# HGRN2 pairs in one tile of two PSUM banks, block states for both heads, alternating sums, and the query norm beside epsilon

## The chip, the cores and the metric

The kernel runs on one core of a Trainium2 chip, as one launch. The metric is the device time of an execution in microseconds; where several executions were timed, their median. Engines are named as in the profile: PE is TensorE (matmul), DVE is VectorE, ACT is ScalarE, POOL is GpSimd and SP is SyncE, which issues most transfers.

## What is computed

A trunk of two layers over 512 positions of width 1024, all in float32. Each layer is a half-step feed-forward block (FFN), a mixer, and a second FFN; a final norm follows.

```python
for layer in range(DEPTH):
    x = x + 0.5 * swiglu(rmsnorm(x, norm_ffn1[layer]), ffn1_gate[layer], ffn1_up[layer], ffn1_down[layer])
    x = x + hybrid_mixer(rmsnorm(x, norm_mix[layer]), ...)
    x = x + 0.5 * swiglu(rmsnorm(x, norm_ffn2[layer]), ffn2_gate[layer], ffn2_up[layer], ffn2_down[layer])
```

The mixer projects x once and runs three kinds of heads on the result. HGRN2 has four heads of key width 64 and value width 64, the gated delta net (GDN) four heads of width 128, and RG-LRU a recurrence over 256 channels:

```python
# HGRN2: S_t = diag(f_t) S_{t-1} + k_t v_t^T (k = 1 - f), o_t = S_t^T q_t
scores = jnp.einsum('bhtd,bhsd,bhtsd->bhts', qi, ki, decay)
o = jnp.einsum('bhts,bhsv->bhtv', scores, vi) + jnp.einsum('bhtd,bhdv->bhtv', qi * jnp.exp(cum), state)
# GDN: the query is scaled to unit length, the output to unit mean square
cq = l2norm(cq) * (GD_DK ** -0.5)
o_gd = o_gd * lax.rsqrt(jnp.mean(o_gd * o_gd, axis=-1, keepdims=True) + EPS) * gd_norm_w * silu(gd_z)
# RG-LRU: two gates of a block-diagonal product, then a scan
r = sigmoid(einsum(xb, wr) + br);  ig = sigmoid(einsum(xb, wi) + bi)
```

## The kernel before

Everything lies transposed, channels in the 128 partitions and the 512 positions (S) in the columns, in four blocks of 128 positions (NJ = 4). A wide product takes a 128x128 weight block against 512 columns into one PSUM bank. To keep float32 accuracy at the fast rate each weight is split into a high part (`whi`, a cast on ACT, L176) and a low part (`wlo`, a difference on DVE, L177), and each step is three products (L212 to L214).

PSUM has eight banks, handed out under three tags: "mm" (three), "mx" (three) and "hx" (two). `bank()` takes the next bank of a tag, in the order in which the program asks, so a request waits for an earlier request of its tag. `rstd` (L293) sums squares on PE and `spread` (L304) spreads a row over the partitions with a product; both take "hx", as do the FFN's down products.

An FFN multiplies gate tiles (mm) and up tiles (mx) and then down tiles. In the very first, the first gate and the first up tile are asked for together and multiplied in turn, k by k, as the pieces of x come in. Which instruction stands where is decided by a tile scheduler, from dependencies and estimated costs, except on PE within the mixer: there the order is written out by a slot scheduler of the kernel (`Slots`), which sets the products of small steps (HGRN2, GDN, RG-LRU) between the wide products of the projection. An engine works its instructions off in order, so a PE instruction that waits holds up all behind it.

HGRN2 works on pairs of heads (two pairs, i = 0 and 1), a head's 64 key rows in each half of the partitions. Scores between positions are built by levels (`hgrn_level`, H = 0, 1, 2, 4, ..., 64): at each level q and k are multiplied with decays (L993, L994), the products of all four blocks are formed for both heads (L1009 for the masked levels, else L1022; e is the head, each has a bank of "hx"), and the part of the result that belongs to the level is copied into the head's score matrix `SD`, by a predicated copy per head on DVE (L1013). `hgrn_state` forms the state products (L1046, the heads alternating between column halves of one bank) and the states at the block starts. `hgrn_sum` adds scores times values (L1064) and state times query (L1067), all blocks of one head and then of the other:

```python
for e in range(2):
    for j in range(NJ):
        m = nc.tensor.matmul(po[r, js], lhsT=V[:, j, vs], rhs=d["SD"][e][:, j, :], ...)
        if j:
            m = nc.tensor.matmul(po[r, js], lhsT=st[r, j - 1, :], rhs=d["q"][r, js], ...)
```

`rglru` forms for each i = 0 and 1 two gate products (L1163), each in a bank of its own, with a Sigmoid on ACT behind each (L1164). `gdn_core` forms the decay masks `DT` with four products (L637) and an Exp each (L639).

Of the kernel before, what the change touches and what calls it, by code (L numbers as in the profile page):

```python
# [112 lines left out]
class Trunk:  # L113
# [14 lines left out]
    def bank(self, tag="mm", shape=(P, S)):  # L128
        return self.tile(self.pp, shape, F32, tag, 2 if tag == "hx" else 3)
# [159 lines left out]
    def rstd(self, j0, n, tag="hx"):  # L289
# [9 lines left out]
    def spread(self, rt, n, tag="hx"):  # L299
# [10 lines left out]
    def ffn(self, l, f, nxt):  # L310
# [6 lines left out]
        for h in range(3):  # L317
# [4 lines left out]
            for kind, m in ffn_order(h):  # L322
# [191 lines left out]
    def mixer_in(self, l):  # L514
# [7 lines left out]
        pv = [self.bank("mx" if j < 2 else "hx", (P, NV)) for j in range(NJ)]  # L522
# [178 lines left out]
    def gdn_q(self):  # L701
# [5 lines left out]
        self.rq = self.tile(self.mp, (P, 16), F32, "rq")  # L707
        rq = self.small(16, "rq_hc")
        self.rsqrt(rq, qsq.rearrange("p h c -> p (h c)"), 16, 1.0, EPS)
        nc.vector.tensor_copy(self.rq.rearrange("p (c h) -> p h c", h=4), rq.rearrange("p (h c) -> p h c", h=4))  # L710
# [130 lines left out]
    def gdn_core(self):  # L841
# [103 lines left out]
    def in_hf(self, l, i):  # L945
# [3 lines left out]
        def then(ps):  # L949
            if i == 0:  # L950
                d = {t: self.tile(self.mp, (P, n), F32, "hg_" + t)
                     for t, n in (("f", S), ("k", S), ("q", S), ("s0", S), ("s1", S), ("kk", 384), ("st", 192))}
            else:

                v = self.tile(self.mp, (P, 4, S), F32, "gd_v")
                d = {t: v[:, j, :] for j, t in enumerate(("f", "k", "q", "s0"))}
                d.update({t: self.tile(self.mp, (P, n), F32, "hg1" + t) for t, n in (("s1", S), ("kk", 384), ("st", 192))})
            d["SD"] = [d[t].rearrange("p (j t) -> p j t", t=P) for t in ("s0", "s1")]
            d["tot"] = d["f"]
            self.hg[i] = d  # L960
# [19 lines left out]
    def hgrn_level(self, i, H):  # L980
# [3 lines left out]
        q, k = d["q"], d["k"]  # L984
        if H == 1:
            nc.vector.tensor_tensor(q, q, d["f"], ALU.mult)
        elif H > 1:

            nb, h = S // H, H // 2
            tv = d["tot"].rearrange("p (b two) -> p b two", two=2)  # L990
            q4 = q.rearrange("p (b two h) -> p b two h", two=2, h=h)
            k4 = k.rearrange("p (b two h) -> p b two h", two=2, h=h)
            nc.vector.tensor_tensor(q4[:, :, 1, :], q4[:, :, 1, :], bc(tv[:, :, 0], h), ALU.mult)  # L993
            nc.vector.tensor_tensor(k4[:, :, 0, :], k4[:, :, 0, :], bc(tv[:, :, 1], h), ALU.mult)  # L994
            t2 = self.tile(self.mp, (P, 256), F32, "hg_tot", bufs=4)[:, 0:nb]
            nc.vector.tensor_tensor(t2, tv[:, :, 0], tv[:, :, 1], ALU.mult)
            d["tot"] = t2
        if H == P:
            return
        if H in MASKED:  # L1000

            nb = P // (2 * H)
            half = lambda v: v.rearrange("p (j b two h) -> p j b two h", j=NJ, b=nb, two=2)[:, :, :, 1, :]
# [342 lines left out]
```

## Time and profile before

| what | value |
| --- | --- |
| median of three runs | 2093.62 us (2089.04 to 2094.09) |
| profiled execution | 2088.65 us |
| its span, first to last instruction | 2086.6 us |
| PE busy | 2063.3 us, 99% |
| DVE busy | 1118.8 us, 54% |
| ACT busy | 807.2 us, 39% |
| mean granted PE clock | 0.996 |

Span and profiled execution differ by 2.05 us, which lie outside the first and the last instruction. Busy time of PE counts a product that is still running, so 99% means that PE almost never waits, and not that it works at its peak.

### The profile page before, as it was taken

What the parts mean: (1) busy time and instruction counts of PE and PEld (TensorE: products, weight loads), DVE (VectorE), ACT (ScalarE), POOL (GpSimd) and SP (SyncE); (2) the same over time, 40 slices, a digit from 0 to 9 for tenths busy, and PEclk for the clock granted to TensorE, in tenths of its full rate; (3) what the DMA queues carried; (4) which work ended last, traced back from release to release, by engine and by line L of the source; (5) the groups of instructions that cost most, each with busy time, mean ns of one, the idle gap of its engine ahead of it and who ended that gap; (6) DMA issues with size and microseconds to landing.
All of it is one profiled execution on the core that took longest, in us unless ns stands there. A gap on an engine that the chain in (4) does not pass through costs nothing.

```text
span 2086.6 us, 26732 instructions
## 1 busy us (share of the span) xinstructions
PE 2063.3 (99%) x10292; PEld 1676.2 (80%) x10292; DVE 1118.8 (54%) x2100; ACT 807.2 (39%) x1533; POOL 12.6 (1%) x38
## 2 busy tenths in 40 slices
PE   8999999999999999999999999999999999999997
PEld 6888888878888888888888888888788878888886
DVE  6434445786676443444644344457856754444345
ACT  5323223644564332323433232346346543223233
POOL 0000000000000000000000000000000000000000
PEclk9999999999999999999999999999999999999999
DMA  5232232322122222322223323223211222332222
GB/s 185 91 100 93 92 100 76 97 71 57 52 64 92 97 91 94 99 91 96 96 91 92 100 91 99 91 74 101 70 39 62 76 91 96 91 100 93 92 90 71
DMA packets 67488, 184.99 MB, mean 89 GB/s; under 512 B 18976, under 2 KB 21920, under 8 KB 67360
## 3 DMA queue, kind: packets, MB, share of 16 engines
q1 hardware_dynamic: 66128, 182.12, 27.3%
q8 instruction: 81, 1.33, 0.3%
q10 hardware_dynamic: 1232, 1.16, 0.2%
q14 instruction: 47, 0.39, 0.1%
HBM read 180.36 MB, written 2.88 MB: 88 GB/s over the span
## 4 chain that ended last, share of the span: by engine, by line
PE 98%; DVE 1%; DMA 0%; issue 0%; ACT 0%; DVEq 0%; SPq 0%; ACTq 0%
PE mm L212 14%; PE mm L214 14%; PE mm L213 14%; PE mx L212 8%; PE mx L214 8%; PE mx L213 8%; PE hx L212 8%; PE hx L214 8%; PE hx L213 8%; PE hx L1009 1%; PE mx L648 1%; PE hx L1064 1%; PE hx L1067 0%; PE mx L637 0%; PE mx L894 0%; PE mx L782 0%
## 5 line engine op out<-in xcount | busy, mean ns | idle before, releaser
L176 ACT CAST whi<-wraw 128x512 fp32r<-128x512 f32 (+2 forms) x696 | 420.3, 606 | 1001.9 <-PE mm L213 361.7
L177 DVE TENSOR_TENSOR wlo<-wraw,whi 128x512 fp32r<-128x512 f32 (+2 forms) x696 | 464.8, 669 | 347.3 <-ACT whi L176 344.5
L212 PE MATMUL mm<-xh,whi 128*128 128x512 f32 x1120 | 456.0, 407 | 6.7 <-ACT whi L176 6.7
L214 PE MATMUL mm<-xh,wlo 128*128 128x512 f32 x1120 | 442.3, 395 | 0.0
L213 PE MATMUL mm<-xl,whi 128*128 128x512 f32 x1120 | 442.0, 395 | 0.0
L212 PE MATMUL mx<-xh,whi 128*128 128x512 f32 x704 | 278.7, 396 | 0.0
L214 PE MATMUL mx<-xh,wlo 128*128 128x512 f32 x704 | 278.5, 396 | 0.0
L213 PE MATMUL mx<-xl,whi 128*128 128x512 f32 x704 | 276.8, 393 | 0.0
L212 PE MATMUL hx<-y,whi 128*128 128x512 f32 x692 | 272.5, 395 | 0.0
L214 PE MATMUL hx<-y,wlo 128*128 128x512 f32 x692 | 272.3, 393 | 0.0
L213 PE MATMUL hx<-y,whi 128*128 128x512 f32 x692 | 272.1, 393 | 0.0
L212 PEld LDWEIGHTS mm<-xh,whi 128*128 128x128 f32 x1120 | 211.2, 189 | 55.2 <-ACT whi L176 6.7
L214 PEld LDWEIGHTS mm<-xh,wlo 128*128 128x128 f32 x1120 | 211.3, 189 | 50.1 <-DVE wlo L177 0.2
L213 PEld LDWEIGHTS mm<-xl,whi 128*128 128x128 f32 x1120 | 211.9, 189 | 45.9 <-issue 1.4
L214 PEld LDWEIGHTS mx<-xh,wlo 128*128 128x128 f32 x704 | 132.4, 188 | 32.1 <-issue 0.7
L213 PEld LDWEIGHTS mx<-xl,whi 128*128 128x128 f32 x704 | 132.7, 189 | 30.9 <-issue 0.2
L212 PEld LDWEIGHTS mx<-xh,whi 128*128 128x128 f32 x704 | 132.5, 188 | 31.1 <-issue 1.0
L213 PEld LDWEIGHTS hx<-y,whi 128*128 128x128 f32 x692 | 130.2, 188 | 30.9 <-DVE y L236 1.1
L214 PEld LDWEIGHTS hx<-y,wlo 128*128 128x128 f32 x692 | 130.0, 188 | 30.6
L212 PEld LDWEIGHTS hx<-y,whi 128*128 128x128 f32 x692 | 130.0, 188 | 29.5
L359 DVE SCALAR_TENSOR_TENSOR x<-hx,x 128x512 f32<-128x512 f32 x94 | 65.0, 692 | 133.1 <-PE hx L214 133.1
L342 DVE TENSOR_TENSOR fu<-mx,rb 128x512 f32<-128x512 f32 x88 | 60.9, 692 | 139.7 <-PE mx L214 139.7
(325 smaller groups left out, 1779.9 us busy)
## 6 DMA issues: line engine op xcount, KB each, us to landing
wraw<-in_wgu SPq DMA_DIRECT2D x176, 512.0 KB, 3.7
wraw<-in_wd SPq DMA_DIRECT2D x64, 512.0 KB, 3.5
wraw<-in_win SPq DMA_DIRECT2D x52, 512.0 KB, 3.5
wraw<-in_wd SPq DMA_DIRECT2D x32, 384.0 KB, 3.0
wraw<-in_wout SPq DMA_DIRECT2D x16, 512.0 KB, 3.5
wraw<-in_wv SPq DMA_DIRECT2D x8, 264.0 KB, 2.6
x<-in_x SPq DMA_DIRECT2D x3, 512.0 KB, 7.7
out_dram<-xw SPq DMA_DIRECT2D x4, 256.0 KB, 2.5
```

The lines of the kernel that those rows point to most:

```text
L176: self.nc.scalar.copy(hi, raw)
L177: self.nc.vector.tensor_tensor(lo, raw, hi.bitcast(F32), ALU.subtract)
L212: nc.tensor.matmul(ps, lhsT=a, rhs=xh, start=(n == 0), stop=False)
L213: nc.tensor.matmul(ps, lhsT=a, rhs=xl, start=False, stop=False)
L214: nc.tensor.matmul(ps, lhsT=b, rhs=xh, start=False, stop=(n == size - 1))
L342: nc.vector.tensor_tensor(u, pu, rb, ALU.mult)
L359: nc.vector.scalar_tensor_tensor(xm, pd, 0.5, xm, ALU.mult, ALU.add)
L648: self.nc.tensor.transpose(ps[:, c, :], v[:, c * P:(c + 1) * P], self.ident)
L1009: nc.tensor.matmul(banks[e][:, j], lhsT=k[r, j * P:(j + 1) * P], rhs=half(q)[r, j], start=True, stop=True)
L1064: m = nc.tensor.matmul(po[r, js], lhsT=V[:, j, vs], rhs=d["SD"][e][:, j, :], start=True, stop=(j == 0))
```

## The change

Two of the PSUM banks become one tile of two banks, under the tag "hx", of which there is one (`pair()`). All that was in "hx" moves. `rstd`, `spread` and half of the FFN's down products go to "mx", the other half to "mm". HGRN2's two heads lie in the two halves of the pair tile, so that one predicated copy serves both heads at each level; q and k share one tile and are decayed by one multiplication; both heads' score matrices share one tile. The states become block diagonal, 128x128 for both heads, zeroed by POOL, and the sums go block by block, the heads in turn, with one state product for both. RG-LRU's two gate products of one i go into the two halves of a pair tile. GDN's query norm is not taken as a reciprocal root of its own; its square sum joins the output's as an epsilon under one root (`qe`).

```diff
     def bank(self, tag="mm", shape=(P, S)):
-        return self.tile(self.pp, shape, F32, tag, 2 if tag == "hx" else 3)
+        return self.tile(self.pp, shape, F32, tag, 3)
+
+    def pair(self):
+
+        return self.tile(self.pp, (P, 2, S), F32, "hx", 1)
...
-    def rstd(self, j0, n, tag="hx"):
+    def rstd(self, j0, n, tag="mx"):
...
-    def spread(self, rt, n, tag="hx"):
+    def spread(self, rt, n, tag="mx"):
...
-                    pd = self.bank("hx")
+                    pd = self.bank(("mm", "mx")[mt % 2])
...
-        self.rsqrt(rq, qsq.rearrange("p h c -> p (h c)"), 16, 1.0, EPS)
-        nc.vector.tensor_copy(self.rq.rearrange("p (c h) -> p h c", h=4), rq.rearrange("p (h c) -> p h c", h=4))
+        self.qe = self.tile(self.mp, (P, 16), F32, "qe")
+        nc.vector.tensor_scalar(self.qe.rearrange("p (c h) -> p h c", h=4), qsq, EPS, P * P * EPS, ALU.add, ALU.mult)
...
-        nc.vector.tensor_tensor(osq, osq, self.rq, ALU.mult)
-        nc.vector.tensor_tensor(osq, osq, self.rq, ALU.mult)
+        nc.vector.tensor_tensor(osq, osq, self.qe, ALU.add)
         ro = self.tile(self.mp, (P, 16), F32, "ro")
-        self.rsqrt(ro, osq, 16, 1.0 / P / P, EPS, float(np.float32(P ** -0.5)))
-        nc.vector.tensor_tensor(ro, ro, self.rq, ALU.mult)
+        self.rsqrt(ro, osq, 16, 1.0 / P, 0.0)
...
-            banks = [self.bank("hx", (P, NJ, nb, H)) for _ in range(2)]
+            pt = pt[:, :, 0:P // 2].rearrange("p g (b h) -> p g b h", h=H)
             for j in range(NJ):
                 for e in range(2):
                     r = slice(64 * e, 64 * e + 64)
-                    nc.tensor.matmul(banks[e][:, j], lhsT=k[r, j * P:(j + 1) * P], rhs=half(q)[r, j],
+                    nc.tensor.matmul(pt[:, NJ * e + j], lhsT=k[r, j * P:(j + 1) * P], rhs=half(q)[r, j],
                                      start=True, stop=True)
-            for e in range(2):
-                sd = half(d["SD"][e].rearrange("p j t -> p (j t)"))
-                nc.vector.copy_predicated(sd, lv[:, None].to_broadcast([P, NJ, nb, H]), banks[e])
+            nc.vector.copy_predicated(half(sd), lv[:, None].to_broadcast([P, 2 * NJ, nb, H]), pt)
...
+        po = self.pair()[:, 0, :]
+        for j in range(NJ):
+            js = slice(j * P, (j + 1) * P)
+            for e in range(2):
+                r = slice(64 * e, 64 * e + 64)
+                nc.tensor.matmul(po[r, js], lhsT=V[:, j, (2 * i + e) * 64:(2 * i + e) * 64 + 64], rhs=sd[:, e, j, :],
+                                 start=True, stop=(j == 0))
+            if j:
+                nc.tensor.matmul(po[:, js], lhsT=st[:, j - 1, :], rhs=d["q"][:, js], start=False, stop=True)
...
+            pr = self.pair()
             for n, cb, s in ((0, C_BR, r[:, i, :]), (1, C_BI, ig)):
-                ps = self.bank("hx")
+                ps = pr[:, n, :]
                 nc.tensor.matmul(ps, lhsT=self.rgw[:, l, n, i, :], rhs=xc, start=True, stop=True)
                 nc.scalar.activation(s, ps, AF.Sigmoid, bias=col(cb + i))
```

How the built programs differ is seen in the order of an engine's instructions. A row gives the line, the operation, what is written and read, and the shape of what is written; some rows name in brackets the engines for whose semaphores the instruction waits. Lines are those of each kernel itself: a product of L212 to L214 before is one of L216 to L218 now.

The first piece is PE at the gate products of RG-LRU in the first layer (hx are their banks, tmp is the input, rgw the weights). Before:

```order
L882 MATMUL mx_916_4794<-gt_913_4769,Kn_593_3079 128x128 [waits Activation_49] x4
L894 MATMUL mx_918_4801<-gt_913_4769,DT_610_3162 128x128 x4
L1163 MATMUL hx_921_4813<-tmp_903_4726,rgw_6_89 128x512 [waits DVE_49]
L1163 MATMUL hx_922_4816<-tmp_903_4726,rgw_6_89 128x512
L212 MATMUL mm_923_4821<-xh_7_91,whi_907_4743 128x512
```

and now:

```order
L887 MATMUL mx_888_4726<-gt_885_4701,Kn_592_3078 128x128 [waits Activation_49] x4
L899 MATMUL mx_890_4733<-gt_885_4701,DT_609_3161 128x128 x4
L1171 MATMUL hx_893_4745<-tmp_875_4658,rgw_6_89 128x512 [waits DVE_49]
L1171 MATMUL hx_893_4745<-tmp_875_4658,rgw_6_89 128x512 [waits Activation_49]
L216 MATMUL mm_894_4752<-xh_7_91,whi_879_4675 128x512
```

The order is the same, the two products share a tile, and the second waits for ACT, which it did not.

The second piece is PE at the start of the program (mm_37 is the first gate tile, mx_38 the first up tile, mm_52 the second gate tile; L293 and L297 are the sum of `rstd`, L304 and L308 the product of `spread`). Before, the first two tiles go in turn for 48 rows, of which two steps are shown, and the sum stands after seven rows of the second gate tile:

```order
L212 MATMUL mm_37_176<-xh_7_91,whi_10_96 128x512
L213 MATMUL mm_37_176<-xl_8_92,whi_10_96 128x512
L214 MATMUL mm_37_176<-xh_7_91,wlo_11_97 128x512
L212 MATMUL mx_38_177<-xh_7_91,whi_40_180 128x512
L213 MATMUL mx_38_177<-xl_8_92,whi_40_180 128x512
L214 MATMUL mx_38_177<-xh_7_91,wlo_41_181 128x512
...
L214 MATMUL mm_52_255<-xh_7_91,wlo_46_191 128x512
L212 MATMUL mm_52_255<-xh_7_91,whi_45_190 128x512
L293 MATMUL hx_21_143<-cst_5_87,ssq_9_93 128x1 x4
```

Now the first gate tile's 24 rows stand alone, eight rows of the second gate tile follow, the sum, 15 rows more, the spread product, and only then the first up tile:

```order
L218 MATMUL mm_37_176<-xh_7_91,wlo_13_103 128x512
L216 MATMUL mm_52_255<-xh_7_91,whi_45_190 128x512
...
L217 MATMUL mm_52_255<-xl_8_92,whi_45_190 128x512
L297 MATMUL mx_21_143<-cst_5_87,ssq_9_93 128x1 x4
L218 MATMUL mm_52_255<-xh_7_91,wlo_46_191 128x512
...
L217 MATMUL mm_52_255<-xl_8_92,whi_47_194 128x512
L308 MATMUL mx_30_167<-sq_29_165,cst_5_87 128x512
L216 MATMUL mx_38_177<-xh_7_91,whi_40_180 128x512
```

Ahead of the spread product 75 wide products stood before (48, 7 and 20), and 47 stand now (24, 8 and 15).

The third piece is DVE in the first layer's levels (hg_s0 and hg_s1 are the score matrices of the two heads of pair 0, hg_sd both; tmp are passes of a convolution; gt and solve belong to GDN). Before:

```order
L1013 COPY_PREDICATED hg_s0_703_3585<-cst_5_87,hx_735_3749 128x256
L752 TENSOR_TENSOR gt_670_3441<-gt_670_3441,solve_682_3474 128x5x11
L492 SCALAR_TENSOR_TENSOR tmp_734_3742<-tmp_733_3739,par_2_76,tmp_734_3742 128x512
L750 TENSOR_TENSOR solve_683_3477<-gt_668_3430,gt_670_3441 128x4x12
L492 SCALAR_TENSOR_TENSOR tmp_734_3742<-tmp_733_3739,par_2_76,tmp_734_3742 128x512
L752 TENSOR_TENSOR gt_670_3441<-gt_670_3441,solve_683_3477 128x4x12
L492 SCALAR_TENSOR_TENSOR tmp_734_3742<-tmp_733_3739,par_2_76,tmp_734_3742 128x512
L750 TENSOR_TENSOR solve_684_3480<-gt_668_3430,gt_670_3441 128x3x13
L1013 COPY_PREDICATED hg_s1_704_3586<-cst_5_87,hx_736_3750 128x256
```

and now:

```order
L1015 COPY_PREDICATED hg_sd_699_3580<-cst_5_87,hx_724_3729 128x512
L755 TENSOR_TENSOR solve_679_3469<-gt_666_3428,gt_668_3439 128x6x10
L496 SCALAR_TENSOR_TENSOR tmp_723_3722<-tmp_722_3719,par_2_76,tmp_723_3722 128x512
L757 TENSOR_TENSOR gt_668_3439<-gt_668_3439,solve_679_3469 128x6x10
L496 SCALAR_TENSOR_TENSOR tmp_723_3722<-tmp_722_3719,par_2_76,tmp_723_3722 128x512
L755 TENSOR_TENSOR solve_680_3472<-gt_666_3428,gt_668_3439 128x5x11
L496 SCALAR_TENSOR_TENSOR tmp_723_3722<-tmp_722_3719,par_2_76,tmp_723_3722 128x512
L757 TENSOR_TENSOR gt_668_3439<-gt_668_3439,solve_680_3472 128x5x11
L1015 COPY_PREDICATED gd_v_645_3359<-cst_5_87,hx_732_3759 128x32x16
```

The copy of both heads stands ahead of the three passes; behind them stands the copy of the next level of pair 1 (gd_v).

## Rows read from the trace of the kernel before

**Rows 1.** The page: span, and an engine's busy time.

```profile
span 2086.6 us, 26732 instructions
PE 2063.3 (99%) x10292; PEld 1676.2 (80%) x10292; DVE 1118.8 (54%) x2100; ACT 807.2 (39%) x1533; POOL 12.6 (1%) x38
```

**Rows 2.** Waits of PE: total us, times, longest.

```profile
PE hx L1009 <- DVE gt L752: 4.0, 2, 2.0
```

**Rows 3.** Busy time by stretches; after POOL's stand clock, DMA share, GB/s.

```profile
462.06:464.33 2.27, 0.28 (x2) 0.14 (x3) 2.27 (x8) 0.63 (x1) 0.10 (x1) 1.00 0.01 4
...
465.13:468.55 3.42, 3.42 (x12) 2.27 (x12) 2.68 (x9) 0.44 (x1) 0.00 (x0) 0.50 0.24 77
```

**Rows 4.** Timeline of PE, RG-LRU's gates: start, us, what.

```profile
563.51 1.88 PE L1163 MATMUL hx<-tmp,rgw 128*128 128x512 f32 x4
...
573.49 1.88 PE L1163 MATMUL hx<-tmp,rgw 128*128 128x512 f32 x4
```

**Rows 5.** Timeline of ACT, the same place.

```profile
565.63 1.28 ACT L1164 ACT_TABLE_LOAD   x1
566.92 0.69 ACT L1164 ACTIVATE y<-hx,par 128x512 f32<-128x512 f32 x1
...
577.48 0.69 ACT L1164 ACTIVATE y<-hx,par 128x512 f32<-128x512 f32 x1
```

**Rows 6.** Timeline of all engines at the kernel's start.

```profile
14.51 1.41 DVE L281 SCALAR_TENSOR_TENSOR xl<-x,par,xh 128x512 fp32r<-128x512 f32 x2
...
18.54 1.13 ACT L176 CAST whi<-wraw 128x512 fp32r<-128x512 f32 x2
...
21.68 0.95 PE L293 MATMUL hx<-cst,ssq 128*128 128x1 f32 x8
...
22.74 0.68 DVE L177 TENSOR_TENSOR wlo<-wraw,whi 128x512 fp32r<-128x512 f32 x1
...
25.33 0.39 PE L213 MATMUL mm<-xl,whi 128*128 128x512 f32 x1
...
25.56 0.40 PE L214 MATMUL mm<-xh,wlo 128*128 128x512 f32 x1
...
27.20 1.02 PE L304 MATMUL hx<-sq,cst 128*128 128x512 f32 x2
```

**Rows 7.** Timeline of DVE and PE at the levels' long wait.

```profile
460.58 0.73 DVE L1013 COPY_PREDICATED hg_s<-cst,hx 128x256 f32<-128x256 int32 x1
...
461.90 0.43 PE L1009 MATMUL hx<-gd_v 64*128 64x64 f32 x2
...
462.78 0.75 DVE L492 SCALAR_TENSOR_TENSOR tmp<-tmp,par,tmp 128x512 f32<-128x512 f32 x1
...
463.55 0.72 DVE L1013 COPY_PREDICATED hg_s<-cst,hx 128x256 f32<-128x256 int32 x1
...
464.33 1.25 PE L1009 MATMUL hx<-gd_v 64*128 64x64 f32 x14 [1.99 <-DVE gt L752]
```

**Rows 8.** Timeline of PE: one call of `hgrn_sum`; then L1046.

```profile
499.17 0.65 PE L1064 MATMUL hx<-gd_v,hg_v 128*64 128x128 f32 x4
499.75 0.43 PE L1067 MATMUL hx<-gd_v,hg1st 64*64 64x128 f32 x2
500.11 0.43 PE L1064 MATMUL hx<-gd_v,hg_v 128*64 128x128 f32 x2
...
503.93 0.50 PE L212 MATMUL mm<-xh,whi 128*128 128x512 f32 x1
...
492.66 0.57 PE L1046 MATMUL hx<-hg_v,hg1kk 128*64 128x64 f32 x12
493.16 0.50 PE L212 MATMUL mm<-xh,whi 128*128 128x512 f32 x1
```

**Rows 9.** Timeline of PE, the decay masks' products.

```profile
403.33 3.67 PE L637 MATMUL mx<-gt,cst 128*128 128x512 f32 x8
```

More of the change, by code (lines that the diff above doesn't have):

```diff
@@ L521, in mixer_in @@
         ba = self.tile(self.mp, (P, NJ, 8), F32, "ba")
-        pv = [self.bank("mx" if j < 2 else "hx", (P, NV)) for j in range(NJ)]
+        pv = self.pair()
+        pv = [self.bank("mx", (P, NV)) for _ in range(2)] + [pv[:, j, 0:NV] for j in range(2)]
         for q in range(4):
@@ L1021, in hgrn_level @@
                     r = slice(64 * e, 64 * e + 64)
-                    nc.tensor.matmul(banks[e][a, j, b], lhsT=k[r, j * P + a.start:j * P + a.stop],
+                    nc.tensor.matmul(pt[a, NJ * e + j, b], lhsT=k[r, j * P + a.start:j * P + a.stop],
                                      rhs=q[r, j * P + b.start:j * P + b.stop], start=True, stop=True)
-        for e in range(2):
-            ps, sd = banks[e], d["SD"][e]
-            if H == 0:
-                nc.vector.tensor_tensor(sd, ps, self.ident[:, None, :].to_broadcast([P, NJ, P]), ALU.mult)
-            else:
-                for o in range(0, P, 2 * H):
-                    nc.scalar.copy(sd[o:o + H, :, o + H:o + 2 * H], ps[o:o + H, :, o + H:o + 2 * H])
+        if H == 0:
+            nc.vector.tensor_tensor(st, pt, self.ident[:, None, :].to_broadcast([P, 2 * NJ, P]), ALU.mult)
+        else:
+            for o in range(0, P, 2 * H):
+                nc.scalar.copy(st[o:o + H, :, o + H:o + 2 * H], pt[o:o + H, :, o + H:o + 2 * H])
     def hgrn_state(self, i, V):
@@ L1035, in hgrn_state @@
         d = self.hg[i]
-        kk = d["kk"].rearrange("p (j c) -> p j c", c=P)
-        st = d["st"].rearrange("p (j v) -> p j v", v=64)
-        ps = self.bank("hx", (P, NJ - 1, P))
+        kk, st = d["kk"], d["st"]
+        ps = self.pair()[:, 0, 0:(NJ - 1) * P].rearrange("p (j t) -> p j t", t=P)
         for j in range(NJ - 1):
@@ L1041, in hgrn_state @@
         nc.scalar.copy(kk, ps)
+        nc.gpsimd.memset(st, 0.0)
         yield 2
-        ps = self.bank("hx", (P, NJ - 1, 64))
+        ps = self.pair()[:, 0, 0:(NJ - 1) * 64].rearrange("p (j v) -> p j v", v=64)
         for j in range(NJ - 1):
@@ L1055, in hgrn_sum @@
         d = self.hg[i]
-        st = d["st"].rearrange("p (j v) -> p j v", v=64)
-        po = self.bank("hx", (P, S))
-        for e in range(2):
-            r = slice(64 * e, 64 * e + 64)
-            vs = slice((2 * i + e) * 64, (2 * i + e) * 64 + 64)
-            last = None
-            for j in range(NJ):
-                js = slice(j * P, (j + 1) * P)
-                m = nc.tensor.matmul(po[r, js], lhsT=V[:, j, vs], rhs=d["SD"][e][:, j, :], start=True, stop=(j == 0))
-                self.behind(m, last)
-                if j:
-                    m = nc.tensor.matmul(po[r, js], lhsT=st[r, j - 1, :], rhs=d["q"][r, js], start=False, stop=True)
-                last = m
+        st = d["st"]
+        sd = d["sd"].rearrange("p (e j t) -> p e j t", e=2, t=P)
+        po = self.pair()[:, 0, :]
+        for j in range(NJ):
+            js = slice(j * P, (j + 1) * P)
+            for e in range(2):
+                r = slice(64 * e, 64 * e + 64)
+                nc.tensor.matmul(po[r, js], lhsT=V[:, j, (2 * i + e) * 64:(2 * i + e) * 64 + 64], rhs=sd[:, e, j, :],
+                                 start=True, stop=(j == 0))
+            if j:
+                nc.tensor.matmul(po[:, js], lhsT=st[:, j - 1, :], rhs=d["q"][:, js], start=False, stop=True)
         ot = d["k"]
@@ L1071, in hgrn_sum @@
         yield 2
-        pt = self.bank("hx", (P, NJ, P))
+        pt = self.pair()[:, 0, :].rearrange("p (j t) -> p j t", t=P)
         for j in range(NJ):
@@ L1106, in then @@
         def then(ps):
-            g = self.hgg[i] = self.tile(self.mp, (P, S), F32, ("hg_q", "hg1s1")[i])
+            g = self.hgg[i] = self.hgqk[:, S:] if i == 0 else self.tile(self.mp, (P, S), F32, "hg1f")
             self.nc.vector.tensor_tensor(g, ps, self.rb, ALU.mult)
@@ L1122, in hgrn_out @@
                 self.second((0,))
-            pt = self.bank("hx", (P, NJ, P))
+            pt = self.pair()[:, 0, :].rearrange("p (j t) -> p j t", t=P)
             for j in range(NJ):
```

53 lines of the change are left out of this document (28 added, 25 removed).

## The prediction

> **What bounds the kernel now.** I began with the busy shares of the page: TensorE is busy 2063.3 of 2086.6 us [rows 1], so there is no other engine to relieve, and the change can gain only where TensorE runs badly and lose only where it is made to wait. The table of TensorE's waits came next: beside the first weights and the kernel's end it holds one entry worth having, 4.0 us in two waits, one a layer, of a level product for VectorE [rows 2]. The table by stretches shows what such a wait costs on top. In the stretch of the wait TensorE has 0.28 us of work in 2.27 us; 0.8 us after it resumes, the granted clock reads 0.50 (1.2 instead of 2.4 GHz) for 3.42 us [rows 3]. At half rate that is 1.7 us of work lost, so a wait of 2 us costs 3.7. The second layer repeats both. Then I read every place that the change touches in order of time, and beside it the order of the built programs, which decides what waits for what.
>
> **RG-LRU gates: +14.1 us, and +6.8 us by the clock.** The two gate products of one i were in two banks; TensorE ran them back to back, four rows of 0.43 us, 0.86 us a product [rows 4]. Now both are halves of one tile `pr`. In the changed program the second product has a wait on ScalarE that the row of before has not (first order piece above): the second product writes the tile that the first Sigmoid reads, and is ordered behind it, though the halves are different banks. TensorE's order is written out, so everything behind that product stands still. When does the first Sigmoid end? For i=0 it starts at 566.92, behind four squares and a table load of 1.28 us, and takes 0.69 [rows 5]: 567.61. The second product could have started at 563.51 + 0.86 = 564.37. That is 3.24 us of standstill. For i=1: 577.48 + 0.69 = 578.17 against 573.49 + 0.86 = 574.35, 3.82 us. ScalarE's order up to these Sigmoids is unchanged, and what it does before them waits only for products ahead of the gates, so the standstill is not shortened by itself. Two layers: 2 x 7.06 = 14.1 us. Nothing hides it: TensorE has no slack later to take it up. Bounds: 12 (if the half-tile wait ends with the Sigmoid's start of writing) to 15.
>
> Each of these four standstills is longer than the 2.27 us after which the clock fell [rows 3]. I charge each the same 1.7 us: 6.8 us, bounds 0 and 9.
>
> **Start of the kernel: +7.0 us.** `rstd` and `spread` now take banks of "mx", which are handed out in program order ahead of the first up tile's. So the first up tile (24 products that were interleaved with the first gate tile) can run only behind the spread product (second order piece). The gate tile alone needs the same pieces of x, the last at 14.51 + 1.41 = 15.92 [rows 6], so its 24 rows end by 16.4 whatever runs between them. The next row needs the weight cast that starts at 18.54 and ends half way through its pair, at 19.1: about 2.7 us without work, where before the up products ran. ScalarE's and VectorE's orders there are the same, so the sum product still comes at about 21.7, and the spread product (27.20 before) earlier by two weight splits that leave the chain between them, each about 0.6 of a 0.68 us row: 26.0. By the spread product 75 wide products had run (48 + 7 + 20), now 47 (24 + 8 + 15). The missing 28 at 0.23 us (25.33 to 25.56) are 6.5 us, less 1.2: 5.3 us. The gap of 2.7 us is again longer than the one that made the clock fall: 1.7 us. Bounds 4 (no fall) to 9 (slow rate until the sum product). At the other three norms of an FFN the same 24 products stand ahead of the spread, only of other tiles: 0.
>
> **HGRN2 levels: -3.4 us, and -3.4 us by the clock.** Before, the first head's copy began at 460.58, and the second's stood behind three 512-column conv passes, at 463.55; the second head's next product waited for it until 464.33, from 461.90 on [rows 7]. Now one copy for both heads stands where the first stood (third order piece). At most it takes twice 0.73 us, to 462.04: a wait of at most 0.14. The conv passes then shift by 0.73 and the next level's copy ends near 465.0, where TensorE wants it near 464.5: its 16 short rows and six wide products (1.4) later. So 0.3 us a layer of new waiting is what I expect, 4.0 becomes 0.6, and waits that short had no fall of the clock behind them. Bounds: 0 (the wait only moves one level on) and 7.8 together. The merged masked copies and multiplications cost VectorE less than the pairs; it is idle nearly half the time, so nothing.
>
> **HGRN2 sums: -9.5 us.** One call takes 499.17 to 503.93, 4.76 us, and there are four. Four rows of one shape stand for 0.58 us, two for 0.36 [rows 8]: 0.11 us a row and 0.14 for the change of shape; before there are 12 runs of one shape a call, two of four rows and ten of two. Now the score products alternate between the column halves of the two heads, and three full state products replace six small ones. Do the halves run side by side? L1046 alternates halves in just that way into one bank: 12 rows of 64 columns in 0.50 us (492.66 to 493.16). One after another they would need 12 x 0.055 + 0.14 = 0.80, side by side 0.47. So side by side. The new call: 8 score rows 4 x 0.11 + 0.14 = 0.58, twice 4 rows at 0.36, three state products at 0.36: 2.38 us, half of before, a gain of 9.5 in four calls. Were they not side by side, 3.26 a call and 6.0 in all. The Trainium skill, "TensorEngine Tiling (Array Packing)", Gotcha 1, says that different row tiles cannot use one PSUM bank at the same time; the change puts both heads' sums into one bank, but as column halves, which the rule does not name. If it held for them too, the gain would be the 6.0; L1046 speaks against that.
>
> **Decay masks: +2.0 us.** In ScalarE's new order a SiLU of a conv tile, with a table load before it and one behind, falls between the Exp of the sums and the first Exp of the masks: two loads of 1.28 and a pass of about 0.69 [rows 5], 3.25 us. The four mask products (0.88 us each [rows 9]) go through three banks, so the fourth, due 2.6 us after the first, waits for the first Exp, some 4.0 us after it less what the first product itself comes later. I take 1.0 a layer; bounds 0 and 1.4.
>
> **Nothing:** the query's epsilon (fewer 16-column VectorE operations at the end of the chain), four state passes instead of a copy and two, POOL's zeroing, the shared q/k tile, the FFN's down products in mm/mx. Each lies on an engine with time to spare, ahead of products that come microseconds later; if that cover were gone they would cost under 1 us each.
>
> **The sum** against the profiled execution (2088.65 us, of which 2086.6 are the span): -9.5 - 3.4 - 3.4 + 7.0 + 14.1 + 6.8 + 2.0 = +13.6 us, so 2102.3. The median of the runs is 2093.62, 5.0 above that execution; on it the sum gives 2107.2. I forecast 2107.
>
> **Rivals.** *The clock holds* after the gates and at the start: 8.5 us less, 2099. For it: four waits are no proof from two. Against: they are longer. *Faster: the first Sigmoid is over when the second gate product comes.* Then 14.1 and 6.8 fall away and the sum is -7.3 us, 2086. It decides at one point: the Sigmoid must end by 564.37 instead of 567.61, so ScalarE would have to be 3.2 us earlier, or the chip would have to pass the wait; the squares and the table load stand ahead of it in both orders, so I see no way. *The single pair tile throttles the levels:* before, each head's bank came free alone; now every level of either pair waits for one copy of both heads. If that costs 0.5 us more at half of the 32 hand-overs (eight levels, two pairs, two layers), 8 us more: 2115. The place worked out above gives 0.3 at the tightest hand-over, so it is unlikely. *The heads don't run side by side,* as the Gotcha read widely would have it: 3.5 us more, 2111; L1046 leaves it little chance.
>
> **How the numbers follow.** The forecast 0.55, heads not side by side 0.07, the clock holding 0.20, throttled levels 0.09, faster 0.06, others 0.03. All of the first two, the fourth and the upper part of the clock holding end slower by over 0.3% (6.3 us, about what a measurement of this kernel can tell from no change): 0.80. The lower part of the clock holding (2099 is 0.26% up) counts as the same: 0.14. Faster 0.06. The range reaches down to the clock holding, with the start at its lower bound, 2097, and up to where either the clock costs 9 or the levels begin to throttle, 2115.
>
> **What would show it.** Right: two TensorE waits of over 3 us a layer at the second gate product, released by ScalarE's Sigmoid, each with a stretch at clock 0.50 behind it; a gap near 16.4 to 19.1; `hgrn_sum` calls of 2.4 us; the level wait under 0.5. Wrong: gate products back to back, or those waits at full clock afterwards; sum calls of 3.3; many level waits of half a microsecond.

## The result, and the profile after

The changed kernel takes 2103.28 us in the median of seven runs (2100.31 to 2108.26), the kernel before 2093.62 (seven runs, 2088.97 to 2094.29). The ratio over the executions is 1.006, 95% interval 1.0048 to 1.0073: slower by 0.6%. The two medians alone are 9.7 us apart, a ratio of 1.0046, because before's executions lie in two groups, three near 2089 us and four near 2094, and its median is one of the upper. The profiled execution of the changed kernel took 2103.26 us, 14.6 more than that of before. First the page of it, span and TensorE's busy time:

```profile
span 2101.4 us, 26560 instructions
...
PE 2053.5 (98%) x10268; PEld 1674.3 (80%) x10268; DVE 1112.8 (53%) x2026; ACT 817.1 (39%) x1535; POOL 14.1 (1%) x42
```

TensorE is busy 9.8 us less than before [rows 1] in a span that is 14.8 us longer, so 24.6 us more are spent without work. The waits of TensorE in the changed kernel (line that waits, releaser, total us, times, longest) say where:

```profile
PE hx L1171 <- ACT y L1172: 13.6, 4, 3.7
PE mm L216 <- ACT whi L180: 8.7, 2, 6.8
PE mx L633 <- DVE g L624: 7.7, 2, 3.9
PE mx L308 <- DVE sq L306: 3.9, 1, 3.9
PE hx L1013 <- DVE gt L757: 2.0, 2, 1.0
PE hx L1023 <- ACT gt L659: 1.5, 2, 0.8
...
PE hx L1013 <- DVE hg_sd L1026: 1.2, 2, 0.6
```

The first line is the gates' second product behind the first Sigmoid. The third is new and was not forecast: the product that sums the decay (L628 before) waits 3.9 us a layer for `g`. L216 holds the first weights (6.8 us) and the gap in the start (2.0); L308 is the spread product of the very last norm, where nothing else is left to do; it waited as long before. The level wait of [rows 2] is spread over three lines, 4.7 us in all. The timelines of TensorE and ScalarE at the gates of the first layer:

```profile
565.82 1.02 PE L1171 MATMUL hx<-tmp,rgw 128*128 128x512 f32 x2
569.97 1.13 PE L1171 MATMUL hx<-tmp,rgw 128*128 128x512 f32 x2 [3.12 <-ACT y L1172]
580.73 1.02 PE L1171 MATMUL hx<-tmp,rgw 128*128 128x512 f32 x2
585.44 2.07 PE L1171 MATMUL hx<-tmp,rgw 128*128 128x512 f32 x2 [3.69 <-ACT y L1172]
```

```profile
567.93 1.28 ACT L1172 ACT_TABLE_LOAD   x1
569.23 0.69 ACT L1172 ACTIVATE y<-hx,par 128x512 f32<-128x512 f32 x1
```

The second product starts as the Sigmoid ends (569.97 against 569.23 + 0.69). The last line of the products took 2.07 us for two rows instead of 1.02: it ran at half rate. The table by stretches (stretch, its length, busy time of PE, PEld, DVE, ACT and POOL, granted clock, DMA share, GB/s) shows where the clock fell and two places where it did not:

```profile
16.93:19.29 2.36, 0.40 (x2) 0.00 (x1) 2.29 (x16) 1.54 (x4) 0.00 (x0) 1.00 0.42 167
...
407.57:414.39 6.82, 5.11 (x11) 3.08 (x12) 4.76 (x11) 4.70 (x6) 0.10 (x1) 0.50 0.01 4
571.41:574.82 3.41, 3.41 (x10) 2.64 (x9) 0.69 (x1) 0.41 (x1) 0.00 (x0) 0.50 0.02 5
585.06:588.47 3.41, 3.03 (x5) 1.81 (x6) 1.17 (x3) 3.36 (x4) 0.00 (x0) 0.50 0.00 0
1445.22:1452.05 6.83, 6.56 (x13) 3.50 (x14) 4.32 (x10) 4.49 (x6) 0.10 (x1) 0.50 0.00 0
1602.64:1609.00 6.36, 3.23 (x12) 1.72 (x11) 3.28 (x6) 4.53 (x13) 0.00 (x0) 1.00 0.01 3
1619.30:1626.12 6.82, 5.46 (x11) 3.69 (x12) 2.63 (x5) 6.56 (x7) 0.00 (x0) 0.50 0.00 0
```

The gap in the start (behind the product of 16.93) stayed at the full clock, and so did the first gate wait of the second layer (1602.64). In the levels it held too, in the second layer as in the first:

```profile
440.00:510.00 70.00, 67.65 (x557) 53.56 (x556) 58.99 (x139) 29.70 (x72) 0.40 (x4) 1.00 0.25 65
```

One call of `hgrn_sum` on TensorE, which answers to [rows 8]:

```profile
506.35 0.66 PE L1065 MATMUL hx<-gd_v,hg_v 128*64 128x128 f32 x8
506.93 0.49 PE L1068 MATMUL hx<-gd_v,hg_st 128*128 128x128 f32 x2
...
508.51 0.49 PE L1068 MATMUL hx<-gd_v,hg_st 128*128 128x128 f32 x2
508.75 0.48 PE L216 MATMUL mm<-xh,whi 128*128 128x512 f32 x1
```

It takes 506.35 to 508.75, 2.40 us against 4.76, and eight score rows stand for the 0.58 us that four stood for: the column halves ran side by side.

**Where the decay comes late.** The wait at L633, on the timeline of TensorE:

```profile
409.28 1.01 PE L633 MATMUL mx<-g,cst 128*128 128x16 f32 x4 [3.87 <-DVE g L624]
```

And what stands ahead of it on VectorE and ScalarE:

```profile
393.52 0.36 DVE L544 TENSOR_SCALAR ba<-hx,rt 128x8 f32<-128x8 f32 x2 [1.09 <-PE hx L540]
...
394.47 0.17 DVE L619 TENSOR_TENSOR g_y<-ba,par 128x16 f32<-128x16 f32 x1
...
395.58 1.28 ACT L646 ACT_TABLE_LOAD   x1
...
396.87 0.22 ACT L646 ACTIVATE beta<-ba 128x16 f32<-128x16 f32 x1
...
397.11 1.28 ACT L408 ACT_TABLE_LOAD   x1
...
398.40 0.22 ACT L408 ACTIVATE sp_z<-sp_a 128x16 f32<-128x16 f32 x1
```

The same two ScalarE steps in the kernel before stood the other way round:

```profile
393.77 0.22 ACT L404 ACTIVATE sp_z<-sp_a 128x16 f32<-128x16 f32 x1
394.01 1.28 ACT L641 ACT_TABLE_LOAD   x1
...
395.30 0.22 ACT L641 ACTIVATE beta<-ba 128x16 f32<-128x16 f32 x1
```

The mixer's four projections of `pv` have blocks j = 2 and 3 in one pair tile now. VectorE's reads of both (L544, one line of two) stand together at 393.52, behind the last product of j = 3. In ScalarE's built order `beta` now stands ahead of the softplus that makes the decay `g`: its table load and the second load behind it, 2.8 us, stand ahead of `sp_z`, which comes 4.6 us later than before. TensorE is only 2.9 us late at that point, by the sum of the mixer's norm, after and before:

```profile
386.55 0.95 PE L297 MATMUL mx<-cst,ssq 128*128 128x1 f32 x8
```

```profile
383.63 0.61 PE L293 MATMUL mx<-cst,ssq 128*128 128x1 f32 x5
```

So 1.7 of the 3.9 us are ScalarE's. The rest is added on VectorE, which computes `g` from `sp_z` in a chain of 16-column steps. `g`, after and before:

```profile
408.96 0.17 DVE L624 TENSOR_TENSOR g<-g_sp,nea 128x16 f32<-128x16 f32 x1
```

```profile
402.29 0.17 DVE L619 TENSOR_TENSOR g<-g_sp,nea 128x16 f32<-128x16 f32 x1
```

From the start of `sp_z` to the end of `g` it takes 10.7 us instead of 8.7: the later chain has eleven 512-column operations between its steps (weight splits and conv passes), where it had seven.

**What was not in the sum.** Three of the four FFNs (the first has the start's loss in it) became faster, by 2.0 to 2.6 us each, with the same products and no wait in them. Two rows of the first product of `rstd` (the second FFN's norm and the next FFN's), before:

```profile
673.47 1.05 PE L293 MATMUL hx<-cst,ssq 128*128 128x1 f32 x8
...
1042.33 1.05 PE L293 MATMUL hx<-cst,ssq 128*128 128x1 f32 x8
```

and after:

```profile
685.74 1.02 PE L297 MATMUL mx<-cst,ssq 128*128 128x1 f32 x8
...
1052.59 1.05 PE L297 MATMUL mx<-cst,ssq 128*128 128x1 f32 x8
```

That is 368.86 us before and 366.85 after. In the trace the starts of neighbouring wide products (mean over the roughly 7,720 pairs under 260 ns apart) lie 230.54 ns apart before and 229.14 after. 1.40 ns x 7,720 = 10.8 us.

### The profile page after: what moved, and what is told of

Read it like the earlier page. It is cut to its first block, busy times and chain, and to the rows that moved or that the text cites. A ratio compares the mean times of both kernels' runs of the same rounds, so it can differ in the third digit from the quotient of the medians.

```text
span 2101.4 us, 26560 instructions
## 1 busy us (share of the span) xinstructions
PE 2053.5 (98%) x10268; PEld 1674.3 (80%) x10268; DVE 1112.8 (53%) x2026; ACT 817.1 (39%) x1535; POOL 14.1 (1%) x42
## 4 chain that ended last, share of the span: by engine, by line
PE 95%; DVE 2%; ACT 1%; issue 0%; DMA 0%; DVEq 0%; SPq 0%; ACTq 0%
PE mm L216 18%; PE mm L218 17%; PE mm L217 17%; PE mx L218 12%; PE mx L216 11%; PE mx L217 11%; PE hx L1013 1%; PE mx L642 1%; PE mx L653 1%; DVE tmp L496 0%; DVE wlo L181 0%; PE mx L899 0%; PE mx L796 0%; PE mx L787 0%; PE mx L679 0%
## 5 line engine op out<-in xcount | busy, mean ns | idle before, releaser
L216 PE MATMUL mm<-xh,whi 128*128 128x512 f32 x1120 | 455.7, 407 | 9.4 <-ACT whi L180 8.7
L218 PE MATMUL mm<-xh,wlo 128*128 128x512 f32 x1120 | 443.3, 396 | 0.2 <-DVE wlo L181 0.2
L216 PE MATMUL mx<-xh,whi 128*128 128x512 f32 x704 | 277.7, 394 | 0.0
L218 PE MATMUL mx<-xh,wlo 128*128 128x512 f32 x704 | 276.7, 393 | 0.0
L216 PEld LDWEIGHTS mm<-xh,whi 128*128 128x128 f32 x1120 | 212.4, 190 | 57.6 <-ACT whi L180 9.2
L218 PEld LDWEIGHTS mm<-xh,wlo 128*128 128x128 f32 x1120 | 211.9, 189 | 48.9 <-DVE wlo L181 0.8
L218 PE MATMUL mm<-y,wlo 128*128 128x512 f32 (+1 forms) x498 | 193.0, 388 | 0.0
L216 PE MATMUL mm<-y,whi 128*128 128x512 f32 (+1 forms) x498 | 192.9, 387 | 0.0
L217 PE MATMUL mm<-y,whi 128*128 128x512 f32 (+1 forms) x498 | 192.6, 387 | 0.0
L216 PEld LDWEIGHTS mx<-xh,whi 128*128 128x128 f32 x704 | 132.2, 188 | 29.9 <-issue 1.0
L218 PEld LDWEIGHTS mx<-xh,wlo 128*128 128x128 f32 x704 | 132.2, 188 | 29.9
L218 PE MATMUL mx<-y,wlo 128*128 128x512 f32 x346 | 136.0, 393 | 0.0
L216 PE MATMUL mx<-y,whi 128*128 128x512 f32 x346 | 135.8, 393 | 0.0
L217 PE MATMUL mx<-y,whi 128*128 128x512 f32 x346 | 135.4, 391 | 0.0
L340 DVE TENSOR_TENSOR fg<-mm,rb 128x512 f32<-128x512 f32 x88 | 60.8, 691 | 136.9 <-PE mm L218 132.3
```

The costliest lines, as they stand in the source:

```text
L216: nc.tensor.matmul(ps, lhsT=a, rhs=xh, start=(n == 0), stop=False)
L217: nc.tensor.matmul(ps, lhsT=a, rhs=xl, start=False, stop=False)
L218: nc.tensor.matmul(ps, lhsT=b, rhs=xh, start=False, stop=(n == size - 1))
L340: nc.vector.tensor_tensor(g, pg, rb, ALU.mult)
```

## The experiments

The theory after the first look: the loss is the gates (some 20 us), the decay (some 12) and the start (5.3); the sums and levels gain about what was forecast; and the closer spacing of the wide products hides part of the loss. The rival for the gates was that the wait, if taken away, would only be met again at the next place, and for the decay that the conv passes delay its chain whatever the tiles are. "Before" was run beside each group of kernels (medians 2091.6, 2091.66 and 2089.57 us).

**Gates' products first** (e1). Both products of an i are written ahead of both Sigmoids, in the same pair tile:

```diff
+            for n in range(2):
+                nc.tensor.matmul(pr[:, n, :], lhsT=self.rgw[:, l, n, i, :], rhs=xc, start=True, stop=True)
             for n, cb, s in ((0, C_BR, r[:, i, :]), (1, C_BI, ig)):
-                ps = pr[:, n, :]
-                nc.tensor.matmul(ps, lhsT=self.rgw[:, l, n, i, :], rhs=xc, start=True, stop=True)
-                nc.scalar.activation(s, ps, AF.Sigmoid, bias=col(cb + i))
+                nc.scalar.activation(s, pr[:, n, :], AF.Sigmoid, bias=col(cb + i))
```

> The changed kernel, with RG-LRU's two gate products of one i written ahead of both Sigmoids; tiles, banks and all else as in the change. Theory: TensorE waits at the second product only because it writes the tile that the first Sigmoid reads. Then the four waits (13.6 us together) and the half-rate stretches behind them (about 6.8 us of work lost) go, and the time falls by some 20 us from 2103, to 2083, the products 0.86 us apart. Rival: the single pair tile itself holds the gates up, or the wait moves to the next user of the tile. Then a wait of 2 to 3 us stands behind the second product or at the next pair tile, and the time stays above 2095.

Measured: 2083.49 us, ratio to before 0.9957 (0.9943 to 0.9971), 19.8 us under the changed kernel. Its waits of TensorE:

```profile
PE mm L216 <- ACT whi L180: 8.9, 2, 6.8
PE mx L633 <- DVE g L624: 7.7, 2, 3.9
```

The gates' line is gone; no other grew by more than 0.3 us, and the one new line is 0.5 us at a decay mask. So 13.6 us of waits and some 6 us of half-rate work hung on the order of two lines of code: the shared tile costs this only where the first reader stands ahead of the second product.

**The decay's projections in tiles of their own** (e2):

```diff
-        pv = self.pair()
-        pv = [self.bank("mx", (P, NV)) for _ in range(2)] + [pv[:, j, 0:NV] for j in range(2)]
+        pv = [self.bank("mx", (P, NV)) for _ in range(2)] + [self.pair()[:, 0, 0:NV], self.bank("mm", (P, NV))]
```

> The changed kernel, with the four value projections of the mixer's start in two mx banks, one half of a pair tile and one mm bank, so that no two of them share a tile. Theory: TensorE's two waits for the GDN decays g (7.7 us) begin there: with two projections in one tile, the third's reads on VectorE and ScalarE come only behind the fourth's products, ScalarE then takes beta's Sigmoid with its table load ahead of the softplus Exp, and the softplus chain on VectorE starts late and runs into the conv passes. Then the waits and their half-rate stretches (6.8 us each) go, and the time falls by about 12 us, to 2091. Rival: the chain is late because the conv passes now stand between its steps whatever the banks are. Then the Exp comes 1.7 us earlier at most, and the time falls by 0 to 4 us, 2099 to 2103.

Measured: 2092.36 us, ratio 1.0007 (0.9996 to 1.0017), 10.9 under the changed kernel; the profiled spans differ by 12.0. The wait alone was 7.7 us; in e2's profiled execution the half rate behind the gates lasted 17.1 us in all against 13.6, which hides part of the gain. Its waits:

```profile
PE hx L1170 <- ACT y L1171: 13.6, 4, 3.7
PE mm L216 <- ACT whi L180: 8.3, 2, 6.8
```

The wait for `g` is gone. On ScalarE's timeline of this run `sp_z` stands ahead of `beta` again:

```profile
396.79 0.22 ACT L408 ACTIVATE sp_z<-sp_a 128x16 f32<-128x16 f32 x1
...
398.32 0.22 ACT L645 ACTIVATE beta<-ba 128x16 f32<-128x16 f32 x1
```

The conv passes are still there, so the rival falls.

**The start in turn again** (e3). `rstd` and `spread` of the FFN take the pair tile, so the first up tile goes in turn with the first gate tile; by the order of requests the PSUM tiles also get the banks they had before:

```diff
-    def rstd(self, j0, n, tag="mx"):
+    def rstd(self, j0, n, tag="hx"):
...
-        ps = self.bank(tag, (P, n))
+        ps = self.pair()[:, 0, 0:n] if tag == "hx" else self.bank(tag, (P, n))
```

(and the same in `spread`).

> The changed kernel, with the banks of rstd and spread taken from the pair tile instead of mx, except in the mixer. The first gate and up tile are interleaved again, as before the change. Theory on the start: the 5.3 us lost there come back, 2098. It also gives the banks the numbers that they had before the change (hx first). Theory on the pace: wide products in the FFN stand 230.1 ns apart since the change and 231.4 before; if bank numbers make that, the pace goes back to 231.4 and some 8 us are lost again, 2106; if not, 230.1 stays.

Measured: 2106.57 us, ratio 1.0065 (1.005 to 1.008), 3.3 over the changed kernel, where the 5.3 us of the start should have come off. The gap in the start is gone, but the wide products lie 230.06 ns apart: 0.92 ns x 7,720 = 7.1 us given back. That makes +1.8 of the 3.3 us; the other 1.5 stay open. The gain that was not in the sum hangs in part on something that this edit undid.

**Down products in turn through mm and mx, in the kernel before** (e4):

```diff
-                    pd = self.bank("hx")
+                    pd = self.bank(("mm", "mx")[mt % 2])
```

> The kernel before, with one line of the change: the FFN's down products alternate between mm and mx instead of using hx. Theory on the pace: six banks in turn instead of two for a third of the products make the wide products 230.1 ns apart instead of 231.4, and the time falls by 8 us from 2093.6, to 2085. Rival: the pace comes from where tiles lie (x and all behind it lie 128 bytes lower since the change, bank numbers moved); then the pace stays at 231.4 and the time is the same, 2093.

Measured: 2091.66 us, ratio 0.9999 (0.9988 to 1.0009), spacing 230.55 ns. The tags of the down products are not the cause.

**Activations 128 bytes back** (e5). The change drops a scratch tile (`rq_hc`) from the small pool, so that x, its high and low parts and all behind them lie 128 bytes lower in SBUF. An unused tile puts them back:

```diff
+            nc.gpsimd.memset(self.small(16, "pad"), 0.0)
```

> The changed kernel with 128 bytes of unused tile put back into the small pool, so that the activations and all that lies behind them in SBUF have the addresses of the kernel before; the order of the PSUM tiles stays that of the changed kernel. Theory one (the wide products' closer spacing, 229.1 ns instead of 230.5, comes from where their operands lie in SBUF): the spacing goes back to about 230.5 and the time rises by some 9 us, to about 2112. Theory two (it comes from which PSUM tiles lie in which banks): the spacing stays at 229.1 and the time at 2103.

Measured: 2119.41 us (2117.93 to 2125.88), ratio 1.0137 (1.0116 to 1.0158): 16.1 us more than the changed kernel. The spacing is 231.13 ns, worse than the 230.54 of before, and 2.0 ns x 7,700 = 15.4 us. The addresses matter, and more than I expected, but the number of before does not come back, so they are not all of it. From sum to sum of `rstd`, as above, this run takes 370.25 us.

**Both repairs** (e6), the edits of e1 and e2 together.

> The changed kernel with both of the repairs that were run singly: the gates' two products written ahead of both Sigmoids, and the four projections of the decay half in tiles of their own. If the two losses are independent (they lie in different stretches of each layer, 20 and 11 us), the time is 2103.3 - 20 - 11 = about 2072. If a part of either was the clock, and the clock's falls only move to other waits when one is taken away, the sum is less: 2076 to 2082.

Measured: 2072.57 us, ratio 0.9903 (0.9885 to 0.992). The two losses add: 19.8 + 10.9 = 30.7, and 2103.28 - 2072.57 = 30.7. That they agree to a tenth is chance: the profiled execution of e6 lost the clock at the start for 6.8 us, which that of the changed kernel did not.

**Three repairs, in the banks of the changed kernel (e7) and in those of before (e8).** The edits of e1, e2 and e3; e7 also asks for an mx and an mm tile ahead of all else.

```diff
+            nc.vector.memset(self.bank("mx", (P, 8)), 0.0)
+            nc.vector.memset(self.bank("mm", (P, 8)), 0.0)
```

> As the run with two repairs, and the first FFN's rstd and spread products again in one pair of banks with the first projections between them, while every PSUM tile lies in the banks of the changed kernel. Theory (the start costs 5.3 us, and the earlier trial of the start alone lost that gain because its PSUM tiles had changed banks): 2072 - 5.3 = about 2067, with the wide products 229.1 ns apart. Rival (the order of the start itself, not the banks, slows the wide products): 230.1 ns apart and about 2074.

> The same instructions as the run with three repairs, with the PSUM tiles in the banks that the start's trial had (and the kernel before). Theory of the banks: wide products 230.1 ns apart, 0.9 ns more over some 7,740 products = 7 us more than the other run with three repairs, about 2074. Rival: no difference, about 2067 or 2074 for both.

Measured: 2072.49 us (ratio 0.9906, 0.9891 to 0.9921), spacing 230.05 ns, and 2071.88 us (0.9904, 0.9889 to 0.9919), 230.08 ns. The two kernels have TensorE's instructions in the same order and, by the order of their requests, different banks: the banks do nothing, and the theory behind e7 and e8 falls. The 0.9 ns come with e3's edit itself, and what it wins at the start it loses again: two repairs and three end at the same time. The edit changes more than the start, though. It also puts the products of `rstd` and `spread` at every FFN norm into the pair tile, and in TensorE's order (e6 against e8) the spread product of the three later ones stands two wide products later. No run separates these from the order of the start.

**Before, with its scratch tile elsewhere** (e9):

```diff
-        rq = self.small(16, "rq_hc")
+        rq = self.tile(self.mp, (P, 16), F32, "rq_hc")
```

> The kernel before, with nothing but the 16-column scratch tile of the query norm (rq_hc) allocated behind the mixer's tiles instead of in the small pool, so that the activations and what lies behind them stand 128 bytes lower, as in the changed kernel. Theory (the spacing of the wide products goes by where their operands lie and by the order of the start, and by nothing else of the change): 230.06 ns, as in the two runs that had these addresses and the interleaved start, 0.48 ns x 7,740 = 3.7 us faster than before, about 2088. Rival (the addresses do nothing by themselves): 230.54 ns and 2091.7.

Measured: 2087.55 us, ratio 0.9975 (0.9963 to 0.9987), spacing 230.04 ns. The kernel before gains a quarter of a per cent from moving a small scratch tile (two buffers of 64 bytes a partition) that takes no part in the wide products. The spacing makes 0.5 ns x 7,736 = 3.9 us of it, 0.19%; the rest goes with the clock, which was granted at 0.998 in three of the ten executions and at 0.996 at most in those of before.

**Three repairs with 128 (e10) and 256 (e11) bytes of unused tile, two repairs with 256 (e12)**, as in e5 with `small(16, ...)` or `small(32, ...)`.

> The run with three repairs, with 128 bytes of unused tile, so that the activations stand where they stood before. The start's order and the activations' addresses are then those of the kernel before. Theory: 230.54 ns and 3.7 us more than without the tile, about 2075.6. Rival (addresses cost 2.0 ns in every order, as they did with the changed start): 232.1 ns and 2088.

> As the run before with 256 bytes of unused tile in place of 128. If the spacing goes by the distance alone (each 128 bytes the same): 231.0 ns, 7 us more than without, 2079. If it goes by which addresses meet, without order: anything from 229 to 232 ns, 2064 to 2087.

> The run with two repairs (gates and projections), with 256 bytes of unused tile. With the changed start 128 bytes made the spacing 231.13 ns instead of 229.13. If each 128 bytes adds the same: 233.1 ns, 31 us more, about 2103. If it goes by which addresses meet, without order: 229 to 232 ns, 2072 to 2095.

Measured: 2075.74 us (ratio 0.9922, 0.9904 to 0.9941), 2071.79 (0.9903, 0.9888 to 0.9918) and 2070.42 (0.9899, 0.9882 to 0.9915); spacings 230.54, 230.04 and 229.13 ns. For e10 that is the spacing of its theory and within 0.2 us of its time; that each 128 bytes adds the same falls with e11 and e12. All kernels together, with the time between the two sums of `rstd` as above:

| order of the start | activations, bytes against before | kernels | mean spacing, ns | sum to sum, us |
| --- | --- | --- | --- | --- |
| in turn | 0 | before, e4, e10 | 230.54 to 230.55 | 368.86 to 369.17 |
| in turn | -128 | e3, e7, e8, e9 | 230.04 to 230.08 | 367.96 to 368.32 |
| in turn | +128 | e11 | 230.04 | 368.32 |
| gate tile alone | -128 | after, e1, e2, e6 | 229.12 to 229.14 | 366.83 to 367.11 |
| gate tile alone | +128 | e12 | 229.13 | 367.11 |
| gate tile alone | 0 | e5 | 231.13 | 370.25 |

Each spacing is that of one profiled execution. Two things fix it to 0.04 ns in all fourteen kernels: the order of the start (or what else e3's edit changes with it), and whether the activations lie where they lay before or 128 bytes to either side. Neither the rest of the change nor the repairs show in it. The fastest version of all, e12, is not to be told from e6, e8 and e11 by its interval.

## Why the prediction was right, and where it was not

The forecast of 2107 and its sign held: 2103.28, and the sum of +13.6 us against +14.8 in the spans. The mechanism at the gates, the sums and the start was right. But that the number came so close is luck: two terms were wrong by some 11 us each, in opposite directions.

| term | forecast, us | measured, us | from |
| --- | --- | --- | --- |
| HGRN2 sums | -9.5 | -9.5 | 4 calls, 4.77 to 2.40 |
| levels and clock behind them | -6.8 | -3.8 | e10, below |
| gates, wait | +14.1 | +13.6 | waits after |
| gates, clock | +6.8 | +6.2 | e1: 19.8 less 13.6 |
| start | +7.0 | +5.3 | 28 products of 0.23, less 1.1 |
| decay | +2.0 | +13.3 | timelines of after and e2, from the mixer's norm to the HGRN2 sums: 6.3 and 7.0 a layer |
| wide products' spacing | 0 | -10.8 | 1.40 ns x 7,720 |
| sum | +13.6 | +14.3 | spans: +14.8 |

**From the profiled execution to the median: a step that failed.** The forecast carried the 5.0 us between before's profiled execution and its median over to the changed kernel. They are not there: its profiled execution took 2103.26 us and its median is 2103.28, so the medians are 9.7 us apart and not 13.6. The run of e4 shows what the 5.0 us can be. Its profiled execution took 2094.65 us, and behind its two level waits the half rate lasted 10.2 us, where before's [rows 3], of 2088.65 us, had 3.4:

```profile
464.48:474.72 10.24, 10.24 (x75) 7.87 (x76) 5.94 (x19) 0.72 (x2) 0.00 (x0) 0.50 0.20 37
1498.71:1508.95 10.24, 10.24 (x75) 7.84 (x74) 6.09 (x20) 1.00 (x3) 0.00 (x0) 0.50 0.28 46
```

6.8 us more at half rate are 3.4 us of work, twice. With the half rate behind the level wait the change removes this too, so on the medians the levels may have been worth some 5 us more than the table says. No execution of before near 2094 us was traced, so this is argued from e4. So +1.2 in the spans and -5.0 here leave the median 3.7 us under the forecast.

**Gates: right,** place, releaser and size. The four waits were 3.1 to 3.7 us. The step on the clock was right in the sum and wrong in its parts: one of the four waits left the clock alone and another was followed by 6.8 us at half rate.

**Sums: right.** Column halves of one bank ran side by side, 2.40 us a call. The Trainium skill, "TensorEngine Tiling (Array Packing)", Gotcha 1, says that different row tiles cannot use one PSUM bank at the same time; it does not name column halves, and no run here tests it on row tiles.

**Start: right in its mechanism,** mis-sized by the clock. The gate tile's last product starts at 16.93 and ends at 17.33 (forecast 16.4), so the gap is 1.96 us and not 2.7, and the spread product comes 1.1 us earlier than in [rows 6] with 28 wide products fewer ahead of it:

```profile
26.08 1.13 PE L308 MATMUL mx<-sq,cst 128*128 128x512 f32 x2
```

The clock did not fall in the profiled execution. In that of e6, which has the same order there and a gap of 2.34 us, it did, for 6.8 us, so this price comes in some executions and not in others:

```profile
21.22:28.04 6.82, 6.82 (x22) 5.67 (x21) 4.08 (x24) 0.62 (x1) 0.00 (x0) 0.50 0.25 80
```

**Levels: half right.** The long wait behind the conv passes is gone and so is the half rate behind it. But the forecast of 0.6 us of new waiting was wrong: 2.0 + 1.5 + 1.2 = 4.7 us in six waits of at most 1.0, where the prediction's own sign was a wait under 0.5. The net is best seen in e10, which has the start's order and the addresses of before. From the decay masks to the sums it takes 403.65 to 497.62, 93.97 us, against 403.33 to 499.17, 95.84 [rows 8, 9]:

```profile
403.65 1.12 PE L641 MATMUL mx<-gt,cst 128*128 128x512 f32 x2
...
497.62 0.66 PE L1064 MATMUL hx<-gd_v,hg_v 128*64 128x128 f32 x8
```

1.9 us a layer. The half rate that is gone makes 1.7 of it; the waits hardly changed, 4.7 us in two layers against 4.4, the line of [rows 2] and this one:

```profile
PE hx L1009 <- DVE hg_s L1027: 0.4, 2, 0.2
```

What won the rest was not traced.

**Decay: the term of the sum that failed.** The prediction saw that ScalarE's order had changed near the decay masks and looked only at the fourth mask product. That wait did not come: L642 has no line among the waits. What came was one product earlier, at the decay's sum, because of a reader two steps up: `pv`'s two blocks in one tile hold the read of the first behind the products of the second, and in the order that the scheduler built with them two ScalarE steps with a table load each have changed places; the chain on VectorE behind them meets four more wide operations. That the tile, and nothing else of the change, turned the order is shown by e2; by which of the scheduler's estimates is not. The prediction followed the pair tile to the gates, the levels and the sums, but not to `pv`, and it asked which TensorE instruction waits for which reader, not which reader comes late. The term was +13.3 instead of +2; the run that took away the shared tile (e2) took away the wait and 10.9 us of the median.

**Wide products: unforeseen.** "Nothing" was claimed for all edits outside the named places. The change moved the activations by 128 bytes and re-ordered the start, and with both together the mean spacing of the wide products is 1.4 ns less, 10.8 us that nearly cancel the decay's error. With the spacing of before the changed kernel would have come to 2103.3 + 10.8 = 2114, near the forecast's upper end; with the addresses of before it came to 2119 (e5), outside the range.

What the change is worth without its losses and without these effects is e10 against before: spans 2074.1 and 2086.6, -12.5 us; sums and levels make -9.5 - 3.8 = -13.3.

## What to carry to other kernels

Two halves of one tile are one thing to the dependency tracker that built this kernel: the product into the second half stood behind the reader of the first (e1), and the reads of the first behind the products into the second (e2), though the halves are different banks. When tiles are merged, write all producers before the first consumer, or keep apart the halves that are produced at different times, and go through every user of the merged tile, on the reading engines too. Before a change of under one per cent is put down to what it computes, compare the spacing of instructions that it did not touch.

## What the runs showed of the hardware that was not expected

- The spacing of the 128x512 products depends on where the activations lie in SBUF. Of the three places tried, 128 bytes apart, the middle one is slower: by 0.5 ns (0.2%) with one order of the start and 2.0 ns (0.9%) with the other, 3.7 and 15.4 us a run. The outer two, 256 bytes apart, do not differ (230.08 and 230.04 ns in e8 and e11, 229.13 in e6 and e12).
- An edit that changes TensorE's order in the first 40 us, and later only the place and the tile of single products at the norms, goes with a spacing that differs by 0.9 ns up to the end of the kernel (229.13 ns in e6, 230.08 in e8). By what it acts stays open; the PSUM banks (e7, e8) and the down products' tags (e4) are ruled out.
- The half rate (granted clock 0.50) behind a wait is no fixed price: stretches of 3.4, 6.8 and, in the run of e4, 10.2 us were seen, and none behind the first gate wait of the second layer (3.1 us, in the stretch from 1602.64).
